# Chunks of seven products at a unit's first and third place, their x sums a chunk later, squares of x over two chunks

## The chip, the cores and the metric

One core of one Trainium2 chip runs the whole program in one launch. The metric is the device time of an execution in microseconds (us), the median of several runs. The kernel before took 1958.94 us (three runs, 1958.81 to 1959.25).

## The reference, cut to what matters

One encoder layer on x (256 rows, 2048 columns, float32): a SwiGLU feed-forward block (FFN1), a mixer, a second SwiGLU block (FFN2), and a last RMSNorm.

```python
def swiglu(h, w_gate, w_up, w_down):
    return (jax.nn.silu(h @ w_gate) * (h @ w_up)) @ w_down

x = x + 0.5 * swiglu(rmsnorm(x, ffn1_norm), ffn1_w_gate, ffn1_w_up, ffn1_w_down)
h = rmsnorm(x, mix_norm)
z = h @ w_in                  # pool branch a, convolution branch b, gates g_a and g_b from z
x = x + (g_a * a + g_b * b) @ w_out
x = x + 0.5 * swiglu(rmsnorm(x, ffn2_norm), ffn2_w_gate, ffn2_w_up, ffn2_w_down)
out = rmsnorm(x, final_norm)
```

D_MODEL is 2048, D_FF 5632. All weights are float32, some 380 MB, and each is used once.

## The kernel before, in words

**Precision.** A float32 product is made of three products of rounded halves: each operand is split into a high part (a rounded copy, made by ScalarE, ACT) and a low part (the rest, made by VectorE, DVE), and high x high, high x low and low x high are added in PSUM. `hi_lo` (line 152) does a split.

**Units and chunks.** The work is one stream of units; a unit is one block of 1024 weight columns over its whole depth (`Unit`, line 56). A chunk is two depth steps of 128 rows, so two weight tiles of 128 x 1024; a unit of depth 2048 has eight chunks, numbered 0 to 7 here. Gate units of an FFN hold 512 gate and 512 up columns; there are 11 of them (u0 to u10). After u4 and after u8 come two down units (`add_down`) that use the four hidden blocks made so far, and two more end the FFN.

**The loop** (`run`, line 527) issues for each chunk i, in this order: the DMA of chunk i+2 (SP queue, five raw buffers), the split of chunk i+1 (`split_chunk`), the side work registered for i by `at(i, fn)`, and the matmuls of chunk i. Each engine works through its own instructions in the order issued. High and low weight tiles have four buffers each, so the split of chunk i+1 can't start before TensorE (PE) has read chunk i-1.

**Chunks of seven products.** `SEVEN = (0, 3)` (line 42) names the chunks of a unit that are done with seven block products in place of eight (Strassen-Winograd): all FFN gate units but u0, and the first four down units of each FFN. Such a chunk has 21 matmuls where a plain one has 24. On the weight side `split_seven` (line 187) makes four sums of 512 columns on DVE, then splits the first raw tile, the block of three sums (1536 columns) and the second raw tile. On the x side `e_forms` (line 302) makes four sums of 128 x 128 on DVE and splits them (ACT, then DVE). It is called
- by `put` (line 383) for hidden blocks, which transposes the previous gate unit's hidden tile (k0 = 0, then k0 = 2) and splits it. The hidden block of depth chunk c = 2 (u mod 4) + k0/2 also gets its sums if c is in SEVEN: k0 = 0 of u0, u4, u8 (c = 0) and k0 = 2 of u1, u5, u9 (c = 3).
- by `scaled_forms` (line 318): ACT makes a scaled copy y, then come the sums. For FFN1 it is side work of u0 (line 896); for FFN2 it is called by `x_transposed` (line 347), two calls of which are side work of one chunk of the last w_out unit.

Four products (P1, P5, P6, P7) gather in PSUM banks 0 to 3 over the unit's two chunks of seven, three go straight into the result banks 4 to 7. In the chunk after the second one `u.early` (line 224) runs: `gate_early` or `down_early` folds the four banks into two tiles (`shared_parts`, line 424: one ACT copy and four DVE operations), and for gate units registers `put` for the two chunks after that. At a unit's end `gate_done_seven` (line 408) adds those tiles to the result banks (DVE, line 413, two of 1024 columns), applies Silu (ACT) and multiplies (DVE, line 418). This is issued before the split of the next unit's chunk 1, so that split and the one of chunk 2 wait in line behind it on ACT and DVE.

**FFN1's u0** has more side work: the scaled split of x (`first_operand`, line 517), the load of x (`load_x`, line 520), the squares of x on ACT and the root behind them (`finish_rstd`, POOL). Chunk 7 of u0 issues the split for u1's chunk 0.

Of the kernel before, what the change touches and what calls it, by code (L numbers as in the profile page):

```python
# [8 lines left out]
F32 = mybir.dt.float32  # L9
# [4 lines left out]
P = 128  # L14
D = 2048
T = 256
# [10 lines left out]
W2 = 2 * C  # L27
# [11 lines left out]
TAPS_BUSY = 4  # L39

GROUP = 4
SEVEN = (0, 3)

B_P1, B_P5, B_P6, B_P7, B_11, B_12, B_21, B_22 = range(8)

# [1 line left out]
V_N1, V_NM, V_N2 = 0, KD, 2 * KD  # L47
# [34 lines left out]
def encoder_kernel(ctx: ExitStack, tc: tile.TileContext, x, xT, vecs, rows, pool_m,  # L82
# [7 lines left out]
    stg = ctx.enter_context(tc.tile_pool(name="stg", bufs=2))  # L90
# [10 lines left out]
    rstd = [const.tile([P, NT], F32, name=f"rstd{i}") for i in range(4)]  # L101
# [4 lines left out]
    def vcol(base, i):  # L106
        return vec[:, base + i:base + i + 1]
# [5 lines left out]
    def at(i, fn):  # L113

        side.setdefault(i, []).append(fn)
# [12 lines left out]
    def add_unit(u):  # L128
        for cc in range(u.k // 2):
            stream.append((u, cc))  # L130
# [21 lines left out]
    def hi_lo(src, h, l=None):  # L152
        nc.scalar.copy(out=h, in_=src)  # L153
        if l is not None:
            nc.vector.tensor_tensor(out=l, in0=src, in1=h.bitcast(F32), op=ALU.subtract)  # L155
        return h, l
# [133 lines left out]
    def block(pool, tag, dtype, name):  # L290
        return pool.tile([P, 4, T], dtype, tag=tag, name=name)
# [5 lines left out]
    def e_tiles(pool, tag, n):  # L297

        return {c: tuple(pool.tile([P, 4, P], F32R, tag=f"{tag}E{x}{c}", name=f"{tag}E{x}{c}_{n}") for x in "hl")
                for c in SEVEN}  # L300

    def e_forms(dst, even, odd):

        e = stg.tile([P, 4, P], F32, tag="sg", name=f"e{Pos.now}")
        a11, a21, a12, a22 = even[:, :P], even[:, P:], odd[:, :P], odd[:, P:]
        for n, (a, b) in enumerate(((a11, a21), (a21, a22), (a11, e[:, 1, :]), (a12, e[:, 2, :]))):
            nc.vector.tensor_tensor(out=e[:, n, :], in0=a, in1=b, op=ALU.subtract)  # L307
        hi_lo(e, *dst)

    def forms_of(lhs, es):  # L310
        def f(c):
            eh, el = es[c]
            r = {n: (eh[:, q, :], el[:, q, :]) for q, n in enumerate(("E7", "E5", "E6", "E3"))}
            r.update(A11=lhs(2 * c, 0), A12=lhs(2 * c + 1, 0), A22=lhs(2 * c + 1, 1))
            return r
        return f

    def scaled_forms(dst, src, gain_base, k0):

        y = stg.tile([P, 2, T], F32, tag="sg", name=f"y{Pos.now}_{k0}")  # L320
        for j in range(2):
            nc.scalar.activation(y[:, j, :], src[j], AF.Copy, scale=vcol(gain_base, k0 + j))
        e_forms(dst, y[:, 0, :], y[:, 1, :])

    def lhs_of(pairs):
        def f(k, t):
            h, l = pairs[k]
            return h[:, t * P:(t + 1) * P], l[:, t * P:(t + 1) * P]
        return f
# [17 lines left out]
    def x_transposed(dst, gain_base, k0, es=None):  # L347

        b = transposes(lambda j, t: X[t][:, (k0 + j) * P:(k0 + j + 1) * P], 2, f"xt{Pos.now}_{k0}")
        for j in range(2):  # L350
            scaled_split(dst[k0 + j], b[:, j * T:(j + 1) * T], vcol(gain_base, k0 + j))
        if es and k0 // 2 in es:
            scaled_forms(es[k0 // 2], [b[:, j * T:(j + 1) * T] for j in range(2)], gain_base, k0)

    def squares(t, slot, c0, c1):
        for n, c in enumerate(range(c0, c1, C)):
            junk = stg.tile([P, C], F32, tag="sg", name=f"sq{Pos.now}_{t}_{c}")
            nc.scalar.activation(junk, X[t][:, c:c + C], AF.Square,  # L358
                                 accum_out=ss[:, t, slot + n:slot + n + 1])

    def finish_rstd(dst):
        nc.vector.tensor_reduce(out=msq, in_=ss, axis=mybir.AxisListType.X, op=ALU.add)
        nc.vector.tensor_scalar(out=msq, in0=msq, scalar1=1.0 / D, scalar2=EPS,
                                op0=ALU.mult, op1=ALU.add)
        nc.gpsimd.tensor_tensor(dst, msq, mhalf, op=ALU.pow)
# [11 lines left out]
    def ffn_units(w_g, w_d, xt, xE, rs, residual_done, tail=None):  # L377
# [5 lines left out]
        def put(u, hs, k0, b=None):  # L383
            b = transposes(lambda j, t: hs[t][:, (k0 + j) * P:(k0 + j + 1) * P], 2, f"hT{Pos.now}_{k0}", b)
            hi_lo(b.rearrange("p (q t) -> p q t", q=2), *(h[:, k0:k0 + 2, :] for h in ffn["ht"][u % GROUP]))
            c = (u % GROUP) * 2 + k0 // 2
            if c in SEVEN:
                y = stg.tile([P, 2, T], F32, tag="sg", name=f"hy{Pos.now}_{k0}")
# [19 lines left out]
        def gate_done_seven(u):  # L408
            def done(acc):
                hs = []  # L410
                for t in range(NT):
                    z = ffn[f"t{t}"]
                    nc.vector.tensor_tensor(out=z, in0=acc[t], in1=z, op=ALU.add)  # L413
                    nc.scalar.activation(z[:, 0, :], z[:, 0, :], AF.Silu, scale=rs[:, t:t + 1])
                for t in range(NT):
                    z = ffn[f"t{t}"]
                    h = hidden_tile(t)
                    nc.vector.scalar_tensor_tensor(out=h, in0=z[:, 1, :], scalar=rs[:, t:t + 1],
                                                   in1=z[:, 0, :], op0=ALU.mult, op1=ALU.mult)
                    hs.append(h)  # L420
                waiting.append((u, hs))
            return done
# [23 lines left out]
        def down_early(half):  # L446
            def early():
                shared_parts()
                for t in range(NT):
                    at(Pos.now + 1 + t, lambda t=t: into_residual(t, half, ffn[f"t{t}"]))  # L450
            return early

        def down_done(half, last):
            def done(acc):
                for t in range(NT):
                    into_residual(t, half, acc[t])
                    if last:
                        squares(t, 2 * half, half * W2, (half + 1) * W2)
                if last:
                    residual_done(half)  # L460
            return done
# [6 lines left out]
        def add_down(g, k, last):  # L468
            for half in range(2):
# [3 lines left out]
                else:  # L473
                    add_unit(Unit(w_d[half], k, hidden_lhs, down_done(half, False), k0=g * GROUP * 4,
                                  forms=forms_of(hidden_lhs, LateE()), early=down_early(half), seven=SEVEN))

# [5 lines left out]
        for u in range(units):  # L482
            if u:
                add_unit(Unit(w_g[u], KD, lhs_of(xt), gate_done_seven(u), forms=forms_of(lhs_of(xt), xE),
                              early=gate_early, seven=SEVEN, start=(lambda: None) if u == 1 else None))
            else:
# [17 lines left out]
    xE1 = e_tiles(xtp, "x", 1)  # L504
# [14 lines left out]

    def load_x(t):  # L520
        nc.sync.dma_start(out=X[t], in_=x[t * P:(t + 1) * P, :])
        at(5, lambda: squares(t, 0, 0, D))
        if t == NT - 1:
            at(5, lambda: finish_rstd(rstd[0]))


    def run(first, last):
        for i in range(first, last):
            Pos.now = i
            load(i + PF - 1)  # L530
            split_chunk(i + LEAD)
            for fn in side.pop(i, []):
                fn()
            if mix.get("conv_on"):
                conv_some()
            run_chunk(i)
# [343 lines left out]
    xr = [block(ffn["pool"], f"xr{j}", F32, f"xr{j}") for j in range(4)]  # L880
# [11 lines left out]
    for t in range(NT):  # L892
        at(2 + t, lambda t=t: load_x(t))
    at(KD // 2, lambda: nc.gpsimd.dma_start(out=vec[:, KD:], in_=vecs[:, KD:]))
    for c in SEVEN:
        at(c + 3, lambda c=c: scaled_forms(xE1[c], [xr[c // 2][:, 2 * c % 4 + j, :] for j in range(2)], V_N1, 2 * c))
    run(0, n1)
    ht_stack.close()

# [108 lines left out]
```

## Time and profile before

| | |
|---|---|
| median of three runs | 1958.94 us |
| the profiled execution's own time | 1958.93 us |
| its span, first to last instruction | 1957.1 us |
| matmuls / DVE / ACT busy | 99% / 78% / 50% of the span |
| granted TensorE clock, mean | 0.998 of full |
| DMA | 196 GB/s on average |

A matmul in the trace overlaps the next one: matmuls of 512 columns start about 0.227 us apart, while each is shown as 0.39 us long. So PE's rate is read from the starts, and a stall is a start that comes late. A row of a timeline gives start, duration, engine, line of the code, operation, output and inputs, the count of like instructions merged into it, and in brackets how long the engine sat idle before it and what ended that.

### The profile page before, as it was taken

The numbers are of one execution on the slowest core, as the hardware profiler recorded it, in microseconds if no ns is written. First come the engines' busy times: TensorE is split into PE (matmuls) and PEld (weight loads), VectorE is DVE, ScalarE is ACT, GpSimd is POOL, SyncE is SP. The second block draws the span as 40 slices with busy tenths as digits, with TensorE's granted clock in tenths as the row PEclk, the third lists the DMA queues.
The fourth block names the chain that finished last, engine by engine and source line by source line (L and its number), as shares of the span: only waits on it lengthen the run. The fifth ranks groups of instructions, "written<-read, shape, count | busy, mean of one in ns | idle before, by whom it ended". The sixth has DMA issues, their size and how long they took to land.

```text
span 1957.1 us, 23246 instructions
## 1 busy us (share of the span) xinstructions
PE 1933.4 (99%) x8680; PEld 1598.3 (82%) x8680; DVE 1521.7 (78%) x1762; ACT 979.2 (50%) x1117; POOL 11.0 (1%) x22
## 2 busy tenths in 40 slices
PE   9999999999999999999999999999999999999998
PEld 7788888878888888888888887887888887888886
DVE  6888888888888655888898766588887888888865
ACT  6545544555445455454444545455554455455544
POOL 0000000000000000000000000000000000000000
PEclk9999999999999999999999999999999999999999
DMA  8555666555565556656666555555656565556654
GB/s 314 178 180 191 205 205 203 194 184 191 187 212 190 197 187 200 193 195 213 201 207 199 191 183 180 185 187 179 203 194 214 195 194 182 193 196 203 196 193 149
DMA packets 106145, 383.90 MB, mean 196 GB/s; under 512 B 11920, under 2 KB 12176, under 8 KB 105776
## 3 DMA queue, kind: packets, MB, share of 16 engines
q1 hardware_dynamic: 104688, 378.45, 58.7%
q0 software_dynamic: 1056, 3.83, 0.6%
q8 instruction: 68, 1.11, 0.2%
q14 instruction: 45, 0.37, 0.1%
q10 hardware_dynamic: 288, 0.14, 0.0%
HBM read 380.28 MB, written 2.10 MB: 195 GB/s over the span
## 4 chain that ended last, share of the span: by engine, by line
PE 94%; DVE 3%; ACT 1%; issue 1%; DMA 1%; DVEq 0%; POOLq 0%; ACTq 0%; POOL 0%
PE ps L256 78%; PE ps L277 13%; PE ps L343 1%; DVE wl L155 1%; DVE sum L193 1%; DVE part L413 0%; DVE extl L155 0%; ACT exth L153 0%; ACT wh L153 0%; DVE e L307 0%; DMA raw<-in_w_g 0%; PE ps L740 0%; ACT sq L358 0%; DMA xr<-in_xT 0%; PE ps L715 0%
## 5 line engine op out<-in xcount | busy, mean ns | idle before, releaser
L153 ACT CAST wh<-raw 128x1024 fp32r<-128x1024 f32 (+1 forms) x706 | 729.2, 1049 | 729.5 <-PE ps L256 361.6
L155 DVE TENSOR_TENSOR wl<-raw,wh 128x1024 fp32r<-128x1024 f32 (+1 forms) x706 | 846.2, 1219 | 316.4 <-ACT wh L153 312.8
L256 PE MATMUL ps<-wh,xt1h 128*128 128x512 f32 x544 | 169.9, 393 | 1.3 <-ACT wh L153 1.0
L256 PE MATMUL ps<-wh,xt3h 128*128 128x512 f32 x544 | 169.6, 393 | 0.0
L256 PE MATMUL ps<-wl,xt1h 128*128 128x512 f32 x544 | 168.3, 390 | 0.4 <-DVE wl L155 0.3
L256 PE MATMUL ps<-wl,xt3h 128*128 128x512 f32 x544 | 168.1, 390 | 0.3 <-DVE wl L155 0.3
L256 PE MATMUL ps<-wh,xt1l 128*128 128x512 f32 x544 | 167.7, 389 | 0.1
L256 PE MATMUL ps<-wh,xt3l 128*128 128x512 f32 x544 | 167.6, 389 | 0.0
L256 PE MATMUL ps<-wh,xt2h 128*128 128x512 f32 x448 | 138.5, 390 | 0.0
L256 PE MATMUL ps<-wh,xt2l 128*128 128x512 f32 x448 | 138.0, 389 | 0.0
L256 PE MATMUL ps<-wl,xt2h 128*128 128x512 f32 x448 | 137.9, 389 | 0.0
L256 PEld LDWEIGHTS ps<-wl,xt1h 128*128 128x128 f32 x544 | 101.9, 188 | 22.9 <-DVE wl L155 1.6
L256 PEld LDWEIGHTS ps<-wl,xt3h 128*128 128x128 f32 x544 | 101.9, 188 | 22.6 <-DVE wl L155 1.2
L256 PEld LDWEIGHTS ps<-wh,xt1l 128*128 128x128 f32 x544 | 102.0, 188 | 22.0 <-DVE xt1l L335 0.5
L256 PEld LDWEIGHTS ps<-wh,xt3l 128*128 128x128 f32 x544 | 102.1, 188 | 21.7
L256 PEld LDWEIGHTS ps<-wh,xt1h 128*128 128x128 f32 x544 | 100.5, 188 | 22.0 <-ACT wh L153 1.6
L256 PEld LDWEIGHTS ps<-wh,xt3h 128*128 128x128 f32 x544 | 100.5, 188 | 19.6
L155 DVE TENSOR_TENSOR extl<-sum,exth 128x1536 fp32r<-128x1536 f32 x56 | 98.5, 1759 | 22.9 <-ACT exth L153 22.9
L256 PEld LDWEIGHTS ps<-wl,xt2h 128*128 128x128 f32 x448 | 84.1, 188 | 17.6
L256 PEld LDWEIGHTS ps<-wh,xt2l 128*128 128x128 f32 x448 | 84.1, 188 | 17.5
L599 DVE SCALAR_TENSOR_TENSOR conv<-gluT,vec,conv 128x241 f32<-128x241 f32 (+14 forms) x240 | 97.0, 473 | 0.0
L256 PEld LDWEIGHTS ps<-wh,xt2h 128*128 128x128 f32 x448 | 83.3, 188 | 16.7
(237 smaller groups left out, 2852.6 us busy)
## 6 DMA issues: line engine op xcount, KB each, us to landing
raw<-in_w_g SPq DMA_DIRECT2D x350, 512.0 KB, 4.2
raw<-in_w_d SPq DMA_DIRECT2D x176, 512.0 KB, 4.0
raw<-in_w_in SPq DMA_DIRECT2D x112, 512.0 KB, 3.9
raw<-in_w_out SPq DMA_DIRECT2D x32, 512.0 KB, 4.2
raw<-in_w_pp SPq DMA_DIRECT2D x16, 512.0 KB, 3.8
raw<-in_w_cp SPq DMA_DIRECT2D x16, 512.0 KB, 3.6
row<-in_rows POOLq DMA_DIRECT2D x7, 512.0 KB, 4.0
X<-in_x SPq DMA_DIRECT2D x2, 1024.0 KB, 10.1
```

The source lines that it names most:

```text
L153: nc.scalar.copy(out=h, in_=src)
L155: nc.vector.tensor_tensor(out=l, in0=src, in1=h.bitcast(F32), op=ALU.subtract)
L193: nc.vector.tensor_tensor(out=out, in0=a, in1=b, op=ALU.add)
L256: nc.tensor.matmul(u.acc[t + c if u.tail and t else t][:, c, :], lhsT=a, rhs=b[:, c * C:(c + 1) * C], start=(t, c) not in u.begun, stop=k ...
L277: nc.tensor.matmul(ps[:, b, :], lhsT=x_, rhs=w_, start=where not in u.begun, stop=b < B_11 and cc == u.seven[-1] and n == 2)
L343: nc.tensor.transpose(out=b[:, j * T + t * P: j * T + (t + 1) * P], in_=src_of(j, t), identity=ident)
L599: nc.vector.scalar_tensor_tensor(out=dst, in0=src, scalar=w, in1=dst, op0=ALU.mult, op1=ALU.add)
```

## The change

SEVEN becomes (0, 2), the first and the third chunk of a unit. The copy y of `scaled_forms` takes a buffer of another tag ("h", the hidden tiles' one, in place of "sg"), and its sums run one chunk later than the copy. In FFN1's u0 the copies come at chunks 1 and 3 (before: 3 and 6), the squares of the first 128 rows of x at chunk 4 and those of the second at chunk 5 (before: all at 5), and `finish_rstd` at chunk 6 (before: 5).

```diff
-SEVEN = (0, 3)
+SEVEN = (0, 2)
...
     def scaled_forms(dst, src, gain_base, k0):
 
-        y = stg.tile([P, 2, T], F32, tag="sg", name=f"y{Pos.now}_{k0}")
+        y = stg.tile([P, 2, T], F32, tag="h", name=f"y{Pos.now}_{k0}")
         for j in range(2):
             nc.scalar.activation(y[:, j, :], src[j], AF.Copy, scale=vcol(gain_base, k0 + j))
-        e_forms(dst, y[:, 0, :], y[:, 1, :])
+        at(Pos.now + 1, lambda: e_forms(dst, y[:, 0, :], y[:, 1, :]))
...
     def load_x(t):
         nc.sync.dma_start(out=X[t], in_=x[t * P:(t + 1) * P, :])
-        at(5, lambda: squares(t, 0, 0, D))
+        for half in range(2):
+            at(4 + t, lambda half=half: squares(t, 2 * half, half * W2, (half + 1) * W2))
         if t == NT - 1:
-            at(5, lambda: finish_rstd(rstd[0]))
+            at(6, lambda: finish_rstd(rstd[0]))
...
     for c in SEVEN:
-        at(c + 3, lambda c=c: scaled_forms(xE1[c], [xr[c // 2][:, 2 * c % 4 + j, :] for j in range(2)], V_N1, 2 * c))
+        at(c + 1, lambda c=c: scaled_forms(xE1[c], [xr[c // 2][:, 2 * c % 4 + j, :] for j in range(2)], V_N1, 2 * c))
```

What follows from SEVEN without an edit of its own: `early` runs at chunk 3 of a unit (before: 4), `put` at chunks 4 and 5 (before: 5 and 6), and the hidden sums of u1, u5 and u9 are those of c = 2, so they belong to the k0 = 0 call.

## Rows read from the trace of the kernel before

**Rows 1.** The page: busy time and share of two engines, and the granted clock in 40 slices.
```profile
PE 1933.4 (99%) x8680; PEld 1598.3 (82%) x8680; DVE 1521.7 (78%) x1762; ACT 979.2 (50%) x1117; POOL 11.0 (1%) x22
PEclk9999999999999999999999999999999999999999
```

**Rows 2.** What PE waited for: us in total, times, longest.
```profile
PE ps L277 <- DVE part L413: 6.6, 4, 1.7
PE ps L343 <- DVE xt3l L335: 1.7, 1, 1.7
```

**Rows 3.** The chain of waits that ended last: the second chunk of seven (chunk 3) of u1, u2 and u3, u6 and u7 of FFN1, then of u2 and u3, u6 and u7 of FFN2 (with u1's first). Columns: start, duration, what.
```profile
72.69 4.76 PE ps L277 x21
...
115.80 4.76 PE ps L277 x21
...
161.37 4.76 PE ps L277 x21
...
375.03 4.76 PE ps L277 x21
...
420.57 4.76 PE ps L277 x21
...
1335.65 4.76 PE ps L277 x21
...
1381.17 4.76 PE ps L277 x21
...
1594.83 4.76 PE ps L277 x21
...
1640.40 4.76 PE ps L277 x21
```

**Rows 4.** Timeline of DVE from chunk 6 of FFN1's u2 to the start of u3: the last hidden sums, the first weight sum for u3's chunk 0, and the addition at the unit's end.
```profile
136.11 0.62 DVE L307 TENSOR_TENSOR e<-hy,e 128x128 f32<-128x128 f32 x2
...
138.02 0.68 DVE L193 TENSOR_TENSOR sum<-raw,raw 128x512 f32<-128x512 f32 x1
...
145.25 2.35 DVE L413 TENSOR_TENSOR part<-ps,part 128x1024 f32<-128x1024 f32 x2
```

**Rows 5.** Timeline of PE in u3's chunk 0: the last of the shared products, and the first that writes a result bank.
```profile
145.61 0.39 PE L277 MATMUL ps<-exth,xEl 128*128 128x512 f32 x1
147.65 0.50 PE L277 MATMUL ps<-exth,xt1h 128*128 128x512 f32 x1 [1.66 <-DVE part L413]
```

**Rows 6.** Timeline of PE: the first matmul of FFN1's u4.
```profile
188.68 0.39 PE L277 MATMUL ps<-wh,xt1h 128*128 128x512 f32 x1
```

**Rows 7.** Timeline of DVE at the same edge, from u3 to u4: the additions of u3's end, four low tiles (chunks 1 and 2 of u4), the first weight sum for chunk 3.
```profile
187.63 2.47 DVE L413 TENSOR_TENSOR part<-ps,part 128x1024 f32<-128x1024 f32 x2
...
191.84 4.63 DVE L155 TENSOR_TENSOR wl<-raw,wh 128x1024 fp32r<-128x1024 f32 x4 [0.19 <-ACT wh L153]
196.44 0.69 DVE L193 TENSOR_TENSOR sum<-raw,raw 128x512 f32<-128x512 f32 x1
```

**Rows 8.** Timeline of PE from the end of FFN1's u0 to the second chunk of seven of u1.
```profile
51.05 0.61 PE L256 MATMUL ps<-wh,xt1l 128*128 128x512 f32 x2
53.11 0.50 PE L277 MATMUL ps<-exth,xt1h 128*128 128x512 f32 x1 [1.44 <-ACT exth L153]
...
72.53 0.39 PE L277 MATMUL ps<-exth,xt1h 128*128 128x512 f32 x1
```

**Rows 9.** Busy time in 56.5 to 59.5 us: PE, PEld, DVE, ACT, POOL, then the granted clock, the DMA share and GB/s.
```profile
56.50:59.50 3.00, 3.00 (x9) 2.36 (x8) 2.90 (x4) 2.91 (x4) 0.00 (x0) 0.52 0.54 176
```

**Rows 10.** Timeline of DVE in chunks 5 to 7 of FFN1's u0: the reduction of the squares, the x sums, the first weight sum for u1's chunk 0.
```profile
42.31 0.17 DVE L362 TENSOR_REDUCE msq<-ss 128x2 f32<-128x12 f32 x1 [3.78 <-ACT sq L358]
...
46.25 0.49 DVE L307 TENSOR_TENSOR e<-y 128x128 f32<-128x128 f32 x2
...
48.69 0.68 DVE L193 TENSOR_TENSOR sum<-raw,raw 128x512 f32<-128x512 f32 x1
```

**Rows 11.** Timeline of PE at two places where transposes of X for FFN2 stand ahead of a chunk: first eight of them in two groups of four and the matmul after them, then eight in one go and the matmul after them.
```profile
1195.92 0.60 PE L343 MATMUL ps<-ident,X 128*128 128x128 f32 x4
...
1198.61 0.71 PE L256 MATMUL ps<-wh,mAh 128*128 128x512 f32 x2
...
1236.82 1.03 PE L343 MATMUL ps<-ident,X 128*128 128x128 f32 x8
1237.61 0.70 PE L256 MATMUL ps<-wh,xt3h 128*128 128x512 f32 x2
```

**Rows 12.** Timeline of DVE ahead of the first of these: the x sums of one block, and the last scaled split of the next.
```profile
1194.03 0.66 DVE L307 TENSOR_TENSOR e<-y 128x128 f32<-128x128 f32 x2 [0.54 <-ACT y L322]
...
1197.65 0.48 DVE L335 SCALAR_TENSOR_TENSOR xt3l<-ps,vec,xt3h 128x256 fp32r<-128x256 f32 x1 [0.54 <-ACT xt3h L334]
```

**Rows 13.** Groups of instructions of ACT: the squares of X, all of the kernel's (count | busy us, mean ns of one | idle us before).
```profile
L358 ACT ACTIVATE sq<-X 128x512 f32<-128x512 f32 x28 | 17.4, 625 | 20.3 <-DVE X L443 13.1 <-DVE X L815 7.2
```

**Rows 14.** Timeline of DVE in one whole split of a chunk of seven (u2, chunk 3): first weight sum, low tile of the three sums, low tile of the second raw tile with the next chunk's first.
```profile
108.08 0.69 DVE L193 TENSOR_TENSOR sum<-raw,raw 128x512 f32<-128x512 f32 x1
...
112.50 1.76 DVE L155 TENSOR_TENSOR extl<-sum,exth 128x1536 fp32r<-128x1536 f32 x1 [0.41 <-ACT exth L153]
114.18 2.35 DVE L155 TENSOR_TENSOR wl<-raw,wh 128x1024 fp32r<-128x1024 f32 x2
```

**Rows 15.** The DMA issues of the gate units' weights: KB each, median us from issue to landing.
```profile
raw<-in_w_g SPq DMA_DIRECT2D x350, 512.0 KB, 4.2
```

## The prediction
> **What bounds the kernel now.** The busy shares come first: PE is busy all the time at the full clock, DVE for 78% [rows 1]. So only two things can change the time: how many matmuls there are, and the moments at which PE stands still. The change keeps every matmul, so I looked for the stalls. The list of PE's waits names five of them [rows 2], but only by the time that PE waited; what a stall really costs is read from the spacing of equal events in the chain of waits. From one gate unit's second chunk of seven to the next's is 72.69 to 115.80, or 43.11 us, wherever nothing is late; into u3 and u7 of both FFNs it is 45.57, 45.54, 45.52 and 45.57 [rows 3]. **Four stalls, 2.46 + 2.43 + 2.41 + 2.46 = 9.76 us.** A chunk of seven takes 4.76 us there, 0.2267 per matmul, so a plain one of 24 takes 5.44.
>
> Their cause stands in DVE's timeline. In u2's chunk 6 the sums of the hidden block of u1 (c = 3) run until 136.7; only behind them, at 138.02, comes the first weight sum for u3's chunk 0, and behind that whole split the addition at u2's end, at 145.25 [rows 4]. PE has done the 12 shared products at 145.84 and waits for the banks until 147.65 [rows 5]. In the edge u3 to u4, with no hidden sums in front, that addition starts at 187.63, 1.05 before the unit's first matmul at 188.68 [rows 6, 7], and nothing waits.
>
> A fifth stall is where FFN1's u0 meets u1: two matmuls start at 51.05, so the next is due at 51.50; the second chunk of seven is due at 51.50 + 4.76 + 10.88 = 67.14 and comes at 72.53 [rows 8]. **5.39 us**, with a stretch of half clock in it: 0.52 was granted after PE had stood still [rows 9]. DVE is late there twice: it waits 3.78 us for eight squares on ACT, then does x sums from 46.25, and reaches the weight sums at 48.69 [rows 10].
>
> A sixth is at the transposes for FFN2: from the first to the matmul after eight of them is 2.69 us in one place, 0.79 in the other [rows 11], so **1.90 us**. Their bank is read late, by a scaled split at 1197.65 that stood behind x sums begun at 1194.03 [rows 12].
>
> **The change part by part.**
>
> *Hidden sums.* With c = 2 in place of 3 they belong to the first call of `put`, now in chunk 4. Between them and the next unit's split lie chunks 5 and 6, in which DVE has 2.4 us of low tiles in 5.44 us of PE. The four stalls go: -9.76.
>
> *u0 of FFN1.* The sums leave chunk 6: 48.69 - 46.25 = 2.44 us of DVE. Of the eight squares, which hold ACT until 42.3 [rows 10] and so DVE's low tiles for chunk 7, four move to chunk 4 (4 x 0.625, 2.5 us of ACT [rows 13]). Together up to 4.9 us earlier, less about 1 us because the low tiles then wait for buffers that PE frees: 3.9. What is needed: a split ends 114.18 + 1.21 - 108.08 = 7.3 us after its first sum [rows 14], at 56.0; the second raw tile's low half is due at the fifth matmul, 51.50 + 0.9 = 52.4. So 3.6 are enough and all 5.39 go. The other end: if the squares gave nothing, 2.44 leave 1.2 of lateness, so some 4 us gained. I take 5.39, since the idle 3.78 us show DVE held by the squares. Chunks 2 to 5 take the moved work on: about 1.1 us of sums at DVE (0.49 + 0.62 [rows 4, 10]), with their halves behind them, and 2.5 of squares at ACT in chunk 4. That could make the split of chunk 6 late; by the order of issue it ends some 2 us before PE wants it. If that cover were gone, the cost would be the lateness itself, under 2 us. POOL's root moves with the last squares, and its reader, the first Silu, comes behind u0's last matmuls, some 5 us later.
>
> *x sums for FFN2.* The copy y frees the bank at once, and the next block's splits no longer stand behind the sums begun at 1194.03 [rows 12]: -1.90, or -1.7 if the splits, which alternate between ACT and DVE, still end a little late.
>
> *The third chunk's split.* This is the price, and the trace of before does not hold it directly: the split for chunk 2 of seven comes right behind the unit's end. Take the edge from u3 to u4, zero at 188.68 [rows 6, 7]. DVE starts the low tiles of chunk 1 at 191.84, +3.16; two take 2.35 and four 4.63, so the starts are 1.14 apart and one lasts 1.21 [rows 7, 14]; the sum of the next split starts 1.18 after the last. So the first sum for chunk 2 falls at 3.16 + 1.14 + 1.18 = +5.48. The block of three sums has its low half 112.50 + 1.76 - 108.08 = 6.18 after that [rows 14]: +11.66. PE wants it at the eighth matmul of chunk 2: 4.76 + 5.44 + 7 x 0.2267 = +11.79. It is in time by about 0.1 us, at 18 edges (nine in each FFN lie between a gate unit and the next unit with sevens; behind a down unit there is no Silu and no product with it). Cost zero, by the rows; bounds: below zero there is nothing, since PE doesn't wait at this place before; above, 0.2 us at each edge (rival B), or a whole late DVE (rival D).
>
> The Trainium skill (VectorE: DVE Perf Modes, The DRAIN you can't avoid) says that the next operation does not start until the pipe of the one before is empty. The trace differs: the low tiles start 1.14 apart and last 1.21 [rows 7, 14]. By the page two gaps would each be some 0.07 longer, and the margin of 0.13 would be gone.
>
> *The rest, at zero.* `early` and `put` move one chunk ahead, with the same instructions: the third chunk's split ends at 5.48 + 7.3 = +12.8, four low tiles more (chunks 3 and 4) at +17.4, and the folding, four operations as long as a weight sum (0.69), at +20.2. PE comes to chunk 4 at +20.4, and the bank that its transposes need is read first, by +18.1. Without that cover, PE would wait for it at each of 28 units. No DMA is added, none moves past another in SP's queue; a tile of the third chunk is asked for when the first one's low tile is done, lands 4.2 us later [rows 15], around zero, and is wanted at +5.5. The "h" buffers are idle where y takes them.
>
> **Sum:** 9.76 + 5.39 + 1.90 = 17.05 less. The profiled execution took 1958.93 us over a span of 1957.1, and the median is 1958.94, so nothing is to be scaled: 1958.93 - 17.05 = 1941.9.
>
> **The rivals.**
>
> *A, forecast:* all six stalls go, none comes: 1941.9. Chance 0.62.
>
> *B, the edges graze:* the margin of 0.1 is smaller than the readings behind it. If the low half comes 0.1 late and PE loses another 0.1 in starting again (the matmul that ends a wait is shown 0.50 long in place of 0.39 [rows 5]), 18 x 0.2 = 3.6, to 1945.5; with the lower end of u0's gain, 1947. The page's rule above would do just that. For it: the margin. Against it: the chain is made of this trace's own gaps. Chance 0.18.
>
> *C, it doesn't do what it says:* the four stalls come from the load on DVE as a whole and are only put off, and 9.76 stay: 1951.7. For it: DVE's total is unchanged. Against it: the hidden sums that fall into u1 (u0's block, in chunk 5) leave the edge from u1 to u2 without a stall, 72.69 to 115.80 [rows 3]. Chance 0.10.
>
> *D, slower:* DVE doesn't catch up behind a unit's end with the second split so near, and PE waits at the third chunk of every unit. If each of the 18 edges pays what a late DVE cost at u3, 2.44: 44 - 17 = 27 more, 1986. It decides from about 0.9 us of lateness (17.05 / 18), ten times the margin on the wrong side. Chance 0.07. The 0.03 left is for anything else.
>
> **How the numbers follow.** A and B hold 0.80, but B's end is soft, so the range reaches to C as well: 1941.0 (a little below A, for readings of 0.1 at several places) to 1952.0. A measurement here tells 0.2%, 3.9 us, from no change. A, B and C lie under 1955.0, and most of the rest does not: faster 0.90, same 0.03, slower 0.07.
>
> **What would show it.** In the changed kernel's chain of waits all gate units should be 43.1 us apart; PE should have no wait for the additions of line 413 and none at 51 us for the sums' high or low part, and the clock should stay full there; the eight transposes near 1180 should take 0.8 us. In the third chunk of a unit the product with the low sums should follow its neighbours at 0.23 us. A wait there is B if it is a tenth or two, D if it is near 1 us. Waits for line 413 at u3 and u7 would be C. A wait in FFN1's chunk 5 or 6 for a weight tile would show that the moved x sums and squares were put at zero wrongly.

## The result, and the profile after

The changed kernel takes **1945.68 us** (median of four runs, 1945.58 to 1946.32) against 1958.88 for the kernel before on the same chip: a ratio of 0.9935 [0.9918, 0.9952]. The forecast was 1941.9, the range 1941.0 to 1952.0. The profiled execution took 1945.58 us over a span of 1943.8, which is 13.3 less than the span before.

From the page, the answer to [rows 1] and the chain's shares by engine (before: PE 94%, DVE 3%):

```profile
PE 1931.8 (99%) x8680; PEld 1597.5 (82%) x8680; DVE 1520.0 (78%) x1762; ACT 975.7 (50%) x1117; POOL 11.3 (1%) x22
PE 98%; DVE 1%; issue 0%; ACT 0%; DMA 0%; DVEq 0%; POOLq 0%; POOL 0%; ACTq 0%
```

PE and DVE have as many instructions as before, and PE's busy time hardly differs; what has changed is where PE stands still. The waits of PE, and of its weight loads (PEld), in us in total, times, longest (against [rows 2]):

```profile
PEld ps L277 <- DVE extl L155: 4.5, 19, 0.7
PEld ps L277 <- DVE wl L155: 1.3, 3, 0.6
...
PE ps L277 <- DVE extl L155: 0.3, 1, 0.3
PE ps L277 <- DVE wl L155: 0.2, 1, 0.2
```

Lines 413 and 343 no longer stand there. What is new is a wait of weight loads for the low half of the sums: 19 times, but only once is a matmul said to wait for it.

The chain of waits, chunks of seven alone (start, duration): in FFN1 both of u2 and u3, the first of u4 and both of the second down unit behind u4; in FFN2 the first of u3, u4, u7 and u8. This answers [rows 3]:

```profile
96.40 4.76 PE ps L277 x21
...
106.60 4.87 PE ps L277 x21
...
139.62 4.76 PE ps L277 x21
...
149.82 4.85 PE ps L277 x21
...
182.82 4.76 PE ps L277 x21
...
268.30 4.76 PE ps L277 x21
...
278.50 4.76 PE ps L277 x21
...
1353.98 4.76 PE ps L277 x21
...
1397.19 4.76 PE ps L277 x21
...
1611.15 4.76 PE ps L277 x21
...
1654.36 4.76 PE ps L277 x21
```

Two things are to be seen. From unit to unit it is now 43.22 and 43.20 in FFN1, 43.21 and 43.21 in FFN2, and 43.21 from FFN1's u7 to u8 too (396.78 to 439.99 in this chain), so **the four stalls of 2.4 us, in u3 and u7, are gone**. And a unit's third chunk takes 4.85 to 4.87 where the first takes 4.76, except in a unit behind a down unit (278.50): **0.1 us is lost at each of the 18 edges.**

DVE at the edge from u2 to u3 shows the first of these (against [rows 4, 5]): the first addition starts at 138.28, 1.18 ahead of u3's first matmul at 139.46, and the split for u3's chunk 0 (137.14, its last low tile) is over before that matmul.

```profile
137.14 1.22 DVE L155 TENSOR_TENSOR wl<-raw,wh 128x1024 fp32r<-128x1024 f32 x1
138.28 1.22 DVE L413 TENSOR_TENSOR part<-ps,part 128x1024 f32<-128x1024 f32 x1
```
```profile
139.46 0.39 PE L277 MATMUL ps<-wh,xt1h 128*128 128x512 f32 x1
```

The edge from u0 to u1 of FFN1 (against [rows 8, 10]): DVE's last work for chunk 7 of u0 and the first weight sum, then PE.

```profile
42.15 2.36 DVE L155 TENSOR_TENSOR wl<-raw,wh 128x1024 fp32r<-128x1024 f32 x2 [2.01 <-ACT wh L153]
...
45.50 0.69 DVE L193 TENSOR_TENSOR sum<-raw,raw 128x512 f32<-128x512 f32 x1
```
```profile
51.98 0.39 PE L277 MATMUL ps<-exth,xt1h 128*128 128x512 f32 x1
...
62.29 0.39 PE L277 MATMUL ps<-exth,xt1h 128*128 128x512 f32 x1
62.94 0.50 PE L277 MATMUL ps<-extl,xt1h 128*128 128x512 f32 x1 [0.26 <-DVE extl L155]
...
64.07 0.50 PE L277 MATMUL ps<-wl,xt1h 128*128 128x512 f32 x1 [0.17 <-DVE wl L155]
```

The weight sums start at 45.50, which is 6.5 ahead of u1's first matmul where they were 2.8 ahead of its due time of 51.50, so 3.7 earlier; PE runs into u1 at 51.98 with no wait. A smaller wait turned up where none was forecast, in u1's third chunk: two matmuls of it come 0.42 and 0.33 late. No half clock follows; the granted clock (the third figure from the end: 1.00, so 2.4 GHz) is full where 0.52 stood in [rows 9]:

```profile
56.00:60.00 4.00, 4.00 (x19) 3.32 (x18) 3.90 (x6) 1.45 (x2) 0.00 (x0) 1.00 0.76 229
```

The transposes for FFN2 (against [rows 11]) take 0.83 us in one piece, from 1188.17 to the next matmul:

```profile
1188.17 1.07 PE L343 MATMUL ps<-ident,X 128*128 128x128 f32 x8
1189.00 0.71 PE L256 MATMUL ps<-wh,mAh 128*128 128x512 f32 x2
```

**Where the 13.3 us are**, from the starts of PE's matmuls in both traces:

| place | forecast | found |
|---|---|---|
| four stalls at u3 and u7 | -9.76 | -9.76 |
| FFN1, u0 to u1 (1.14 left: 0.11 in u1's first chunk, 1.03 in its third) | -5.39 | -4.25 |
| transposes for FFN2 | -1.90 | -1.86 |
| third chunk, 18 edges at 0.097 | 0 | +1.75 |
| FFN2, u1's third chunk (5.12 in place of 4.76) | 0 | +0.36 |
| start of the program (u1 due at 51.98, before at 51.50) | 0 | +0.48 |
| sum | -17.05 | -13.28 |

### The profile page after: what moved, and what is told of

Its sections match the earlier page's. It is cut to its first block, busy times and chain, and to the rows that moved or that the text cites. A ratio compares the mean times of both kernels' runs of the same rounds, so it can differ in the third digit from the quotient of the medians.

```text
span 1943.8 us, 23272 instructions
## 1 busy us (share of the span) xinstructions
PE 1931.8 (99%) x8680; PEld 1597.5 (82%) x8680; DVE 1520.0 (78%) x1762; ACT 975.7 (50%) x1117; POOL 11.3 (1%) x22
## 4 chain that ended last, share of the span: by engine, by line
PE 98%; DVE 1%; issue 0%; ACT 0%; DMA 0%; DVEq 0%; POOLq 0%; POOL 0%; ACTq 0%
PE ps L256 82%; PE ps L277 13%; PE ps L343 2%; PE ps L741 0%; DVE wl L155 0%; DMA xr<-in_xT 0%; DVE sum L193 0%; PE ps L716 0%; ACT exth L153 0%; ACT wh L153 0%; DVE extl L155 0%; DVE raw L193 0%; ACT fsq L850 0%; ACT sg L401 0%; PE ps L623 0%
```

## The experiments

Each ratio is against the kernel before on the same chip, which took 1958.9 to 1960.1 us (medians); below a microsecond the traces decide, not the times of different chips.

**1. What takes the four stalls away: the place of the sums, or the smaller spacing of the chunks?** Two kernels: the change without its first line, and the kernel before with nothing but its late hidden sums put off.

`seven03`, on the kernel after:
```diff
-SEVEN = (0, 2)
+SEVEN = (0, 3)
```
Expected: 

> The changed kernel with the chunks of seven back at the first and fourth place; the later x sums, the h buffer and the split squares stay. Theory (the sums of the hidden block c = 3, done in chunk 6, hold up the next unit's split): the four stalls of 2.4 us at u3 and u7 come back, +9.8, and what the third place costs goes: 0.1 us at 18 edges, 1.0 at FFN1's u1 and 0.36 at FFN2's u1, so about 1945.7 + 9.8 - 1.8 - 1.4 = 1952.3. FFN1's first edge stays without its stall of 5.4. Rival (the gain came from the x sums and the squares alone): 1945.7 or a little less. Rival (the spacing has nothing to do with the edges' 0.1): 1955.4.

Measured: 1953.36 us, ratio 0.9967 [0.9954, 0.9979], span 1951.9. The waits for line 413 are back with the count, total and longest of [rows 2], and no weight load waits 18 times for the sums:

```profile
PEld ps L277 <- DVE part L413: 8.3, 4, 2.1
PE ps L277 <- DVE part L413: 6.6, 4, 1.7
```

Not foreseen: in u1, whose copy at chunk 4 now has its sums at chunk 5, the first chunk of seven still loses 0.92.

`late_sums`, on the kernel before, in `put`:
```diff
-                e_forms(ffn["hE"][c], y[:, 0, :], y[:, 1, :])
+                if k0:
+                    at(Pos.now + 3, lambda: e_forms(ffn["hE"][c], y[:, 0, :], y[:, 1, :]))
+                else:
+                    e_forms(ffn["hE"][c], y[:, 0, :], y[:, 1, :])
```
Expected: 

> The kernel before with one edit: the sums of the hidden block c = 3 come three chunks later, in the next unit's chunk 1, so that nothing but low tiles stands ahead of the split for the next unit's chunk 0. The places of the sevens stay first and fourth. Theory: the four stalls go without any change of SEVEN, 1958.9 - 9.8 = 1949.1, and no new one comes. Rival (DVE's load as a whole, or the distance between the two chunks of seven, makes the stalls): nothing changes, 1958.9, or the stalls appear elsewhere.

Measured: 1949.94 us, ratio 0.9951 [0.9936, 0.9966], span 1948.1. DVE in u2's chunk 6 and at its end:

```profile
135.08 0.68 DVE L155 TENSOR_TENSOR ht1l<-ps,ht1h 128x512 fp32r<-128x512 f32 x1
135.68 0.68 DVE L193 TENSOR_TENSOR sum<-raw,raw 128x512 f32<-128x512 f32 x1
...
142.91 2.47 DVE L416 TENSOR_TENSOR part<-ps,part 128x1024 f32<-128x1024 f32 x2
```

The weight sum follows the hidden tile's low half at once. The addition starts 26.3 after u2's second chunk of seven (116.64 in this chain), where it was 29.5 [rows 3, 4]; no wait for it is left, and all four stalls are gone, with the chunks of seven at 0 and 3. The stall at u1 and the one at the transposes remain, as in the kernel before. So the stalls came from the sums' place in DVE's line ahead of the next unit's split, not from the load on DVE (rival C) and not from the spacing; the change takes them away by moving the sums.

**2. What loses 0.1 us in the third chunk?** DVE at the edge from u1 to u2 of the kernel after, from the second addition to the low half of the sums:

```profile
96.44 1.23 DVE L413 TENSOR_TENSOR part<-ps,part 128x1024 f32<-128x1024 f32 x1 [0.16 <-PE ps L256]
...
99.40 2.36 DVE L155 TENSOR_TENSOR wl<-raw,wh 128x1024 fp32r<-128x1024 f32 x2 [0.19 <-ACT wh L153]
101.67 0.68 DVE L193 TENSOR_TENSOR sum<-raw,raw 128x512 f32<-128x512 f32 x1
...
106.16 1.76 DVE L155 TENSOR_TENSOR extl<-sum,exth 128x1536 fp32r<-128x1536 f32 x1 [0.49 <-ACT exth L153]
```

With the unit's first matmul at 96.23, the sum starts at +5.44 (forecast +5.48) and the low half ends at 107.92, +11.69 (forecast +11.66); the edge from u3 to u4, which the forecast was made for, has the same two values. PE and PEld there:

```profile
107.80 0.39 PE L277 MATMUL ps<-exth,xEh 128*128 128x512 f32 x1
108.02 0.45 PE L277 MATMUL ps<-extl,xEh 128*128 128x512 f32 x1
108.31 0.40 PE L277 MATMUL ps<-exth,xEl 128*128 128x512 f32 x1
```
```profile
107.57 0.19 PEld L277 LDWEIGHTS ps<-exth,xEh 128*128 128x128 f32 x1
107.97 0.19 PEld L277 LDWEIGHTS ps<-extl,xEh 128*128 128x128 f32 x1 [0.21 <-DVE extl L155]
108.08 0.19 PEld L277 LDWEIGHTS ps<-exth,xEl 128*128 128x128 f32 x1
```

The matmul that reads the low half starts on its time (108.02, +11.79); what came late is the load of the x tile ahead of it. It was due with the matmul before, at 107.80 (+11.57), and waited until 107.97 for an operand that only its matmul reads. The next matmul starts 0.29 later in place of 0.227. Three edits give the low half more room in different ways.

`ext_two`, in `split_seven` (two of the sums split first, so the first low half is ready earlier):
```diff
-        return (hi_lo(r0, *stream_tiles(i, 0)), hi_lo(sm, *ext), hi_lo(r1, *stream_tiles(i, 1)))
+        first = hi_lo(r0, *stream_tiles(i, 0))
+        for q in (slice(0, 2), slice(2, 3)):
+            hi_lo(sm[:, q, :], *(e[:, q, :] for e in ext))
+        return (first, ext, hi_lo(r1, *stream_tiles(i, 1)))
```
Expected: 

> The changed kernel, with the split of the three weight sums in two instructions on each engine (two sums, then the third). DVE and ACT do the same elements in 56 instructions more each. Theory (in the third chunk PE waits about 0.1 us for the low half of the sums, which comes as one piece): two sums' low half ends about 1.0 us earlier, the 18 edges lose their 0.1, -1.75, and u1 gains some of its 1.0 and 0.36: 1942.8 to 1943.9. Rival (the 0.1 is PE's own, or a new instruction costs DVE more than it brings): 1945.7 or more.

Measured: 1943.24 us, ratio 0.9916 [0.9901, 0.9931], span 1941.6. Every edge is at 4.76 (u2's is shown); u1's third chunk in FFN1 still takes 5.03:

```profile
63.13 5.03 PE ps L280 x21
...
106.51 4.76 PE ps L280 x21
```

`low_last`, the order of a block's three products in a chunk of seven (the low half is wanted one matmul later, DVE is untouched):
```diff
-            for n, (x_, w_) in enumerate(((xh, wh), (xh, wl), (xl, wh))):
+            for n, (x_, w_) in enumerate(((xh, wh), (xl, wh), (xh, wl))):
```
Expected: 

> The changed kernel with one edit: in a chunk of seven the three matmuls of each product come as high x high, low x high, high x low, so that the weights' low half is wanted one matmul later, 0.227 us. Theory (in the third chunk the low half of the sums comes about 0.12 us after PE wants to start loading for its matmul, at 18 edges): 0.227 is enough, the chunks of 4.86 us are 4.76 again, -1.75, and the waits in u1 shrink by 0.2 each: about 1943.6. Rival (the 0.1 is a fixed loss of these chunks, not lateness): 1945.7.

Measured: 1943.89 us, ratio 0.9919 [0.9905, 0.9932], span 1941.9. All edges are at 4.76, and the 19 waits of weight loads are one:

```profile
PEld ps L277 <- DVE extl L155: 0.5, 1, 0.5
```

One matmul, 0.227 us, is enough, with the same work on DVE. So the cause is the low half's time against the load, as the rows of PEld had it. (u1's third chunk stays long, 5.64 in FFN1 and 4.90 in FFN2: its low halves are wanted far earlier.)

**3. u1's third chunk.** `order_u1`, in `run` (u1 takes its four shared products first in its third chunk too, as the other units do):
```diff
-        for b, form, wh, wl in own + shared if u.start else shared + own:
+        for b, form, wh, wl in own + shared if u.start and not cc else shared + own:
```
Expected: 

> The changed kernel with one edit: in u1 of each FFN the own products come first in chunk 0 alone. Theory (the order sets the deadline: second and fifth matmul in place of eighth and seventeenth): the waits in the third chunk of u1 go, 1.0 us in FFN1 and 0.36 in FFN2, 1944.3. Rival (the splits are late whatever the order): 1945.7.

Measured: 1944.67 us, ratio 0.9925 [0.9909, 0.9942], span 1942.7. u1's third chunk takes 4.76 in both FFNs, the other edges still 4.83 to 4.89, and 18 weight loads still wait:

```profile
PEld ps L277 <- DVE extl L155: 3.9, 18, 0.2
```

`both` is `ext_two` and `order_u1` in one kernel.

Expected: 

> The changed kernel with the sums' split in two and, in u1 of each FFN, the own products first in chunk 0 alone (they came first in the third chunk too). Theory (u1 loses 1.0 and 0.36 us because its own products want the sums' low half at the second matmul and the second tile's at the fifth, where other units want them at the eighth and seventeenth): all edges and both u1 without a wait, 1945.7 - 1.75 - 1.35 = 1942.6. Rival (u1's loss is DVE's lateness whatever the order): as with the two-part split alone.

Measured: 1942.96 us, ratio 0.9916 [0.9901, 0.9931], span 1941.1. Every chunk of seven takes 4.76 and no matmul or load waits in one. For a comparison on one chip the kernel after, unedited, and `both` were run again side by side, as `after_again` and `both_again`:

Expected of `after_again`: 

> The changed kernel once more, unedited, so that the others of this call are compared with it on the same chip: 1945.7, with about 1 us of difference between chips.

Expected of `both_again`: 

> The kernel with the sums' split in two and u1's order, once more beside the changed kernel. Theory: 3.2 us under the changed kernel of this call (18 edges of 0.1, 1.1 and 0.36 in u1). Rival (it gained nothing over the two-part split or over the changed kernel): within 1 us of it.

Measured: 1945.99 us (1945.88 to 1946.41), ratio 0.9929 [0.9917, 0.9942], and 1942.55 (1942.19 to 1943.08), ratio 0.9911 [0.9896, 0.9926]. The two edits are worth 3.4 us; the places in the table above sum to 1.75 + 1.14 + 0.36 = 3.25. `both` is the fastest kernel here; its two medians are 1.1 and 0.7 us above what was forecast of the change, 1941.9.

**4. The other two parts of the change.** `squares_back` puts all squares of x back into chunk 5:
```diff
-            at(4 + t, lambda half=half: squares(t, 2 * half, half * W2, (half + 1) * W2))
+            at(5, lambda half=half: squares(t, 2 * half, half * W2, (half + 1) * W2))
         if t == NT - 1:
-            at(6, lambda: finish_rstd(rstd[0]))
+            at(5, lambda: finish_rstd(rstd[0]))
```
Expected: 

> The changed kernel with all eight squares and the root back at chunk 5 of FFN1's u0. Theory (the squares held ACT and so the low tiles of chunk 7): the first weight sum for u1's chunk 0, at 45.5 now, comes about 2.4 us later, at 47.9, still earlier than the 48.7 of before, and PE loses 2 to 4 us at FFN1's first edge: 1947.7 to 1949.7. Rival (taking the x sums out of chunk 6 was enough): 1945.7.

Measured (one run): 1948.41 us, span 1946.5. DVE's wait for the squares is back, the first weight sum comes 5.0 ahead of u1's first matmul (48.35 against 53.39) in place of 6.5, and PE waits in u1's first chunk, which takes 6.31 in place of 4.87:

```profile
44.41 0.17 DVE L362 TENSOR_REDUCE msq<-ss 128x2 f32<-128x12 f32 x1 [3.59 <-ACT sq L358]
...
48.35 0.68 DVE L193 TENSOR_TENSOR sum<-raw,raw 128x512 f32<-128x512 f32 x1
```
```profile
54.58 0.50 PE L277 MATMUL ps<-extl,xt1h 128*128 128x512 f32 x1 [0.80 <-DVE extl L155]
```

So the squares' part of the first edge's gain is 1.44 (2 to 4 were expected); that the earlier x sums bring the larger rest is inferred, as no run moves them alone. The span is another 1.4 longer because u1's first matmul comes at 53.39 in place of 51.98, which is no effect of the edit: this execution waited 1.66 for an x tile at the start of u0's chunk 1, at 14.84 (last section). Only with these 1.4 does the time fall into the expected range, which is luck.

`sums_at_once` puts the x sums back behind the copy in the same chunk, from the copy's old buffers:
```diff
-        y = stg.tile([P, 2, T], F32, tag="h", name=f"y{Pos.now}_{k0}")
+        y = stg.tile([P, 2, T], F32, tag="sg", name=f"y{Pos.now}_{k0}")
...
-        at(Pos.now + 1, lambda: e_forms(dst, y[:, 0, :], y[:, 1, :]))
+        e_forms(dst, y[:, 0, :], y[:, 1, :])
```
Expected: 

> The changed kernel with the x sums right behind the copy again, and the copy in its old buffer. Theory (the transposes for FFN2 waited for a bank whose readers stood behind the sums): the wait of 1.9 us comes back there and nowhere else, 1947.5. Rival (the moved places alone took it away): 1945.7.

Measured (one run): 1947.52 us, span 1945.7. The wait of [rows 2] at the transposes is back, 1.68 us in the middle of the eight:

```profile
1187.99 0.60 PE L343 MATMUL ps<-ident,X 128*128 128x128 f32 x4
1190.27 0.66 PE L343 MATMUL ps<-ident,X 128*128 128x128 f32 x4 [1.68 <-DVE xt3l L335]
```

Not foreseen: FFN1's u1 gains. The first weight sum comes 7.39 ahead of u1's first matmul (52.59) in place of 6.48, u1's first chunk loses nothing, and its third takes 5.20 in place of 5.79, from its first matmul to the next chunk's:

```profile
45.20 0.69 DVE L193 TENSOR_TENSOR sum<-raw,raw 128x512 f32<-128x512 f32 x1
```
```profile
62.78 0.40 PE L277 MATMUL ps<-exth,xt1h 128*128 128x512 f32 x1
...
67.98 0.61 PE L256 MATMUL ps<-wh,xt1h 128*128 128x512 f32 x2
```

So putting off the sums brings 1.86 at the transposes and costs 0.7 here: u1 loses 1.14 in the kernel after, 1.12 in `after_again` and 0.44 in this one. That the time meets the expected 1947.5 is chance: u1's 0.7 is made up for by a start that is 0.61 later (52.59 against 51.98, last section). The copy's buffer and the sums' place were put back together, so which of the two does either is not shown.

**5. How near is rival D?** `seven01` leaves no chunk between the two:
```diff
-SEVEN = (0, 2)
+SEVEN = (0, 1)
```
Expected: 

> The changed kernel with the chunks of seven at the first and second place. Theory (the price of a place is the time of the low half of its sums against PE's want of it): the first sum would start about 2.9 us into the unit, the low half end at 9.1, and PE want it at 4.76 + 1.59 = 6.35: 2.75 us late and 0.1 for the restart at 18 edges, 51 us; at the 8 edges behind a down unit about 2.1, 17 us; u1 2.7 and 3.5. Less what the third place cost, 1945.7 + 71 = 2016, and up to 30 more if the waits bring stretches of half clock. Rival (DVE catches up within the chunk, since it is busy 78% only): under 1960.

Measured (one run): 2022.05 us, span 2020.3. At 16 of the 18 edges a pair of chunks of seven takes 12.48 to 12.51 where 9.52 is due, so about 2.97 are lost; at the other two (FFN1's u10, FFN2's u2) it takes 13.62 and 13.45, with the clock granted at 0.50 in part of it (652.3:655.6 and 1362.3:1365.6). Behind down units 1.43 to 1.47 are lost, and in u1 5.4 and 5.0, where 2.7 and 3.5 were expected. Every step of the split is late in turn (second chunk of the first down unit, behind u4):

```profile
244.89 0.50 PE L277 MATMUL ps<-wh,ht1h 128*128 128x512 f32 x1 [0.64 <-ACT wh L153]
246.26 0.50 PE L277 MATMUL ps<-wl,ht1h 128*128 128x512 f32 x1 [0.88 <-DVE wl L155]
...
248.51 0.50 PE L277 MATMUL ps<-extl,hEh 128*128 128x512 f32 x1 [0.61 <-DVE extl L155]
```

The mechanism of D is real: with one plain chunk of 5.44 us between the two an edge loses 0.1, with none it loses 3.

## Why the prediction was right, and where its size was off

- **What bounds the kernel, and the four stalls: right.** Behind the start of the program PE stood still only where a split or an addition came late, and 9.76 us came out to the hundredth. `seven03` brings the stalls back and `late_sums` removes them alone.
- **The transposes: right**, 1.86 of 1.90, and with the sums and the copy as they were (`sums_at_once`) the wait is back.
- **The third chunk's split: the chain right, the deadline wrong.** The low half of the sums was forecast at +11.66 and came at +11.69. "PE wants it at the eighth matmul ... +11.79" is the step that failed: the load ahead of that matmul waits for it as well, one matmul earlier, at +11.57. The margin was not +0.13 but -0.12. This is rival B in place and sign, at half its price: 0.097 per edge in place of 0.2. The matmul itself starts on time, and the loss shows in the spacing behind it. Shown by `low_last` and `ext_two`.
- **The page's rule.** The Trainium skill (VectorE: DVE Perf Modes, The DRAIN you can't avoid) says that the next operation waits until the pipe is empty, and I had noted that by it the margin would be gone. The same paragraph adds that an operation which is not held starts earlier, which I had left out. The rows go with the addition: a low tile shown 1.22 long is followed 1.14 after its start (137.14 and 138.28 above). So the rule is not the reason for the 0.1: the low half came within 0.03 of the forecast, and the 0.1 was lost at the load.
- **FFN1's first edge: 4.25 of 5.39.** The squares and sums did what was said: the weight sums came 3.7 earlier against u1, where 3.9 was forecast, and u1's first chunk lost 0.11 only. What failed is that I took u1's order of products for its first chunk alone. In u1 the own products come first in both chunks of seven, so its third chunk wants the sums' low half at the second matmul and the second raw tile's low half at the fifth. I had costed it like the other units' third chunks, where these are the eighth and the seventeenth. 1.03 in FFN1 and 0.36 in FFN2 went there; `order_u1` removes both.
- **Work put at zero in u0's chunks 2 to 6:** no matmul of u0 waits there, as forecast, nor at `early` and `put` (`put` comes in 20 gate units, where the prediction counts 28 units). But putting this work at nothing failed as well: with the x sums in chunks 1 and 3, not 2 and 4, u1 loses 0.7 less (`sums_at_once`). The 0.48 at the start of the program comes from the first matmuls and not from the change (last section).

Rivals C and D did not occur; what stands against C is now shown, not argued. With 1.75 + 1.14 + 0.36 + 0.48 = 3.73 us on the cost side, the sum of 17.05 becomes the measured 13.3. That 1945.68 is so near to rival B's 1945.5 is chance: the edges make up 1.75 of B's 3.6, and the rest comes from u1 and the start of the program, which B does not have.

## What to carry to other kernels

Before work is split finer or engines are relieved, look for what stands ahead of the critical work in an engine's own line: in `late_sums` a few small sums and their split, put off by three chunks at four places, took away all four stalls, 9.76 us, with DVE's load unchanged. Where a deadline is worked out to a tenth of a microsecond, take it at the weight load ahead of the matmul and not at the matmul, and ask of each unit which order of products it really has. A margin smaller than one matmul is none.

## What the runs showed of the hardware that was not expected

- In this kernel a weight load waits for the operand that only its matmul reads: 0.21 us at 107.97, though the tile that it loads had been used by the load before. One statement of the kernel (line 277) makes both, load and matmul, so whether the chip or the place of the wait in the program holds the load is not shown. The matmul starts on time and 0.1 is lost all the same, in the spacing of 0.23 to 0.29 that follows.
- The start of the program differs from run to run: the first pairs of matmuls are up to 1.1 apart, in place of 0.45, until 7.9 us in the kernel before, 10.1 in the kernel after and 12.4 in `late_sums`. In `late_sums` the granted clock stands at 0.50 of full (1.2 GHz) in 10.5:12 (below); the kernel after has pairs 0.85 apart in 8.5:10, where its clock is shown as 1.00, so the clock's rows do not account for all of it. In `squares_back` the pairs are at their pace by 8.5, but PE waits 1.66 at 14.84. u1 is due between 51.50 and 53.39 accordingly, though no edit touches u0's first chunk: `late_sums`, whose u0 is that of the kernel before, is due at 52.77, the kernel before at 51.50. So kernels a microsecond apart are told apart by their traces sooner than by their medians:

```profile
10.50:12.00 1.50, 1.50 (x5) 1.21 (x4) 0.94 (x1) 0.52 (x1) 0.00 (x0) 0.50 1.04 418
```
